# SwiGLU's second product on one Trainium2 core: seven products of halved operands in place of eight, with the operand sums kept in DRAM

## The chip, the cores and the metric

The program runs on one core of one Trainium2 chip. TensorE (PE) multiplies matrices, VectorE (DVE) and ScalarE (ACT) work on elements, GpSimd (POOL) works on elements and issues transfers, and SyncE (SP) issues transfers. The metric is the device time of one execution in microseconds; less is better.

## The reference

One decoder layer on 1024 tokens of width 1024: a mixer sub-layer, a residual with a layer norm, a SwiGLU sub-layer, and a second residual with a layer norm. Only the last part matters here:

```
def swiglu(u, w1, w2):                      # u: 1024 x 1024
    gate, up = jnp.split(u @ w1, 2, axis=-1)   # w1: 1024 x 5632
    return (jax.nn.silu(gate) * up) @ w2       # w2: 2816 x 1024
# y = layer_norm(ALPHA * x1 + g2 * swiglu(u2), ln2_g, ln2_b)
```

All inputs and the output are float32. The kernel holds each operand of a product as a high and a low part (`split`: ScalarE rounds to float32r, VectorE subtracts), and makes a product of three matmuls: high by high, high by low, low by high.

## The kernel before

The mixer sub-layer takes the first 1300 us and is not touched. Then comes a loop over eight token tiles that writes the normed rows to DRAM (`scratch["n1"]`), then SwiGLU.

**SwiGLU's first product** makes the hidden values h, 2816 by 1024 (hidden by tokens), in 22 blocks of 128 hidden units. The first three blocks are plain. Blocks 3 to 21 (the loop at L1180) already use seven products for eight: gate and up, and the two token halves, are the halves of a 2 by 2 scheme. Each of the seven products of a block is 4 x 3 = 12 matmuls of 128x128 by 128x512 (`product`, L1109). Between them ScalarE and VectorE take sums out of PSUM, and `sums` (L1132 to L1137 and the splits) prepares the next block's weights, in six portions. VectorE must read an accumulator before the next product that adds into it, two products later. The hidden values go to `scratch["h"]` in DRAM (L1210, L1214).

**SwiGLU's second product** goes over two groups of 512 tokens. In a group, 22 steps over the hidden blocks each load w2's rows (128x1024, by SP) and h's block (128x512, by ACT's queue), split both, and issue 24 matmuls (`step`, L1231): four token tiles by two halves of the columns by three. The first four steps (`AHEAD`, L1237) are set up while the first product still runs, with tiles of the older pools; those pools are closed behind them and the new pools `f2a`, `f2`, `f2l` take their memory. The last 4 or 6 steps of a group are done token tile by token tile, so that the ends of the rows are spread out. At a row's end VectorE does, for each half, a product with g2, a sum with the residual and `bn_stats` (L1308 to L1311), then `bn_aggr`, and two scalings for each half (L1316, L1320); the row goes out on SP's queue. The residual rows are loaded from `n1` (L1287) and scaled and shifted in VectorE (L1295).

Within a stage the order on each engine is made by a list scheduler when the program is built, by program order among what it takes to be ready; on the chip each engine then keeps to that order. `tc.issue_after(x)` puts an instruction behind x on its engine. A load can be placed ahead of its place in the program when its memory is free.

## Time and profile before

| | us |
|---|---|
| median of three runs (2087.52 to 2092.55) | 2088.6 |
| the profiled execution, its own time | 2079.7 |
| its span, first to last instruction | 2078.0 |
| PE busy | 2015.1 (97%) |
| DVE busy | 1234.6 (59%) |
| ACT busy | 750.8 (36%) |
| POOL busy | 137.3 (7%) |

Busy times are sums over all stages. A matmul's length in the profile (389 ns) is longer than the time between two starts, since matmuls are pipelined. The difference between the time and the span, 1.7 us, lies before the first and behind the last instruction.

### The profile page before, as it was taken

What the parts mean: (1) busy time and instruction counts of PE and PEld (TensorE: products, weight loads), DVE (VectorE), ACT (ScalarE), POOL (GpSimd) and SP (SyncE); (2) the same over time, 40 slices, a digit from 0 to 9 for tenths busy, and PEclk for the clock granted to TensorE, in tenths of its full rate; (3) what the DMA queues carried; (4) which work ended last, traced back from release to release, by engine and by line L of the source; (5) the groups of instructions that cost most, each with busy time, mean ns of one, the idle gap of its engine ahead of it and who ended that gap; (6) DMA issues with size and microseconds to landing.
All of it is one profiled execution on the core that took longest, in us unless ns stands there. A gap on an engine that the chain in (4) does not pass through costs nothing.

```text
span 2078.0 us, 26649 instructions
## 1 busy us (share of the span) xinstructions
PE 2015.1 (97%) x10254; PEld 1588.5 (76%) x10254; DVE 1234.6 (59%) x2323; ACT 750.8 (36%) x1214; POOL 137.3 (7%) x226
## 2 busy tenths in 40 slices
PE   6999999999999899999999999999999999999998
PEld 5777777776777677776776788788888888878886
DVE  6584575565642767447656457654856565445756
ACT  3514323323325433434445323554333333333231
POOL 1101102001001000002112000010000000000000
PEclk9999989999989999999999999999999999999999
DMA  9111111111121445211111565545423222265552
GB/s 294 48 63 37 44 44 46 46 52 46 56 64 56 147 143 163 62 41 32 35 32 41 170 210 166 178 142 171 142 73 92 91 77 76 76 232 178 185 177 75
DMA packets 195311, 213.20 MB, mean 103 GB/s; under 512 B 10588, under 2 KB 146416, under 8 KB 195184
## 3 DMA queue, kind: packets, MB, share of 16 engines
q1 hardware_dynamic: 162672, 139.51, 22.4%
q10 hardware_dynamic: 30400, 66.70, 9.3%
q0 software_dynamic: 2112, 5.29, 0.8%
q8 instruction: 81, 1.33, 0.3%
q14 instruction: 46, 0.38, 0.1%
HBM read 168.45 MB, written 43.00 MB: 102 GB/s over the span
## 4 chain that ended last, share of the span: by engine, by line
PE 77%; DVE 10%; issue 6%; ACT 4%; DMA 3%; POOL 1%; SPq 1%; DVEq 0%; ACTq 0%; POOLq 0%
PE psd L143 20%; PE accf L1231 11%; PE py L1109 7%; PE pj L143 5%; PE px L1109 5%; PE pz L1109 5%; PE woa L1030 3%; PE pgu L143 3%; PE po L871 2%; PE pt L857 2%; DVE tw L478 1%; DVE TI L480 1%; PE pm L463 1%; PE pss L841 1%; PE pw L530 1%
## 5 line engine op out<-in xcount | busy, mean ns | idle before, releaser
L143 PE MATMUL psd<-ul,wh 128*128 128x512 f32 x992 | 337.8, 411 | 0.7 <-DVE ul L274 0.7
L143 PE MATMUL psd<-uh,wh 128*128 128x512 f32 x992 | 334.6, 409 | 0.3 <-ACT wh L118 0.2
L143 PE MATMUL psd<-uh,wl 128*128 128x512 f32 x992 | 332.0, 407 | 1.1 <-DVE wl L120 1.1
L143 PEld LDWEIGHTS psd<-uh,wh 128*128 128x128 f32 x992 | 185.5, 191 | 40.9 <-issue 6.4
L143 PEld LDWEIGHTS psd<-ul,wh 128*128 128x128 f32 x992 | 183.3, 190 | 41.3 <-issue 6.8
L143 PEld LDWEIGHTS psd<-uh,wl 128*128 128x128 f32 x992 | 184.3, 191 | 39.5 <-issue 5.7
L107 ACT ACTIVATE wh<-wraw 128x1024 fp32r<-128x1024 f32 (+1 forms) x89 | 83.9, 943 | 329.6 <-PE psd L143 252.5
L108 DVE TENSOR_TENSOR wl<-wraw,wh 128x1024 fp32r<-128x1024 f32 (+1 forms) x89 | 95.6, 1074 | 66.9 <-ACT wh L107 64.9
L1231 PE MATMUL accf<-w2h,hh 128*128 128x512 f32 x320 | 105.1, 389 | 1.3 <-ACT w2h L107 1.3
L1231 PE MATMUL accf<-w2l,hh 128*128 128x512 f32 x320 | 105.2, 389 | 0.5 <-DVE w2l L108 0.5
L1231 PE MATMUL accf<-w2h,hl 128*128 128x512 f32 x320 | 105.0, 389 | 0.0
L108 DVE TENSOR_TENSOR w2l<-w2raw,w2h 128x1024 fp32r<-128x1024 f32 x44 | 53.7, 1222 | 35.7 <-ACT w2h L107 30.6
L1231 PEld LDWEIGHTS accf<-w2h,hh 128*128 128x128 f32 x320 | 60.0, 188 | 14.0 <-ACT w2h L107 1.7
L1231 PEld LDWEIGHTS accf<-w2l,hh 128*128 128x128 f32 x320 | 60.0, 188 | 13.4 <-DVE w2l L108 1.0
L1231 PEld LDWEIGHTS accf<-w2h,hl 128*128 128x128 f32 x320 | 60.1, 188 | 12.5
L847 ACT ACTIVATE sc<-sc,mx 128x128 f32<-128x128 f32 (+7 forms) x64 | 49.6, 775 | 42.4 <-DVE mx L846 36.5
L849 POOL TENSOR_SCALAR sc<-sc,mx 128x128 f32<-128x128 f32 (+7 forms) x64 | 48.8, 766 | 218.0 <-DVE mx L848 186.6
L534 ACT ACTIVATE UV<-pu 64x64 f32<-64x64 f32 x64 | 13.7, 214 | 136.6 <-PE pu L533 136.4
L143 PE MATMUL pj<-oh,wh 128*128 128x512 f32 x192 | 59.2, 390 | 0.3 <-DVE macc L974 0.3
L143 PE MATMUL pj<-ol,wh 128*128 128x512 f32 x192 | 59.4, 390 | 0.0
L107 ACT ACTIVATE w2h<-w2raw 128x1024 fp32r<-128x1024 f32 x44 | 46.1, 1051 | 36.7 <-DMA w2raw<-in_ffn_w_dram 18.9
L108 DVE TENSOR_TENSOR hl<-hraw,hh 128x512 fp32r<-128x512 f32 x40 | 27.5, 689 | 53.5 <-ACT hh L107 53.4
(457 smaller groups left out, 4188.6 us busy)
## 6 DMA issues: line engine op xcount, KB each, us to landing
wraw<-in_w_in_dram SPq DMA_DIRECT2D x62, 512.0 KB, 3.9
w2raw<-in_ffn_w_dram SPq DMA_DIRECT2D x44, 512.0 KB, 3.7
w1raw<-in_ffn_w_dram SPq DMA_DIRECT2D x38, 512.0 KB, 4.2
wada<-in_w_ada_dram SPq DMA_DIRECT2D x64, 256.0 KB, 2.9
s_gate<-gate ACTq DMA_DIRECT2D x24, 512.0 KB, 2.9
gate<-s_gate ACTq DMA_DIRECT2D x24, 512.0 KB, 4.3
s_h<-ht ACTq DMA_DIRECT2D x44, 256.0 KB, 2.2
hraw<-s_h ACTq DMA_DIRECT2D x44, 256.0 KB, 3.2
```

Of the source, the lines that this page charges most:

```text
L107: S.activation(hi, raw, AF.Copy)
L108: return V.tensor_tensor(lo_, raw, hi.bitcast(F32), OP.subtract).ins
L143: i = mm(ps[:, h * HF:(h + 1) * HF], w[:, k, :], u[k][h], start=(k == 0 and w is wh and u is uh), stop=(k == nk - 1 and w is wl))
L463: mm(pm[hd][:, :, j], BK[hr, c].rearrange("p a b -> p (a b)"), AR[hr, c], start=True, stop=True)
L478: V.tensor_tensor(t3, X[:, s + 1:32, s:s + 1].to_broadcast([64, ni, nj]), TI[:, s:s + 1, 0:nj].to_broadcast([64, ni, nj]), OP.mult)
L847: S.activation(sc[:, 0:n], sc[:, 0:n], AF.Exp, bias=mx[:, 2:3], accum_out=mx[:, 3:4])
L849: G.tensor_scalar(sc[:, 0:n], sc[:, 0:n], mx[:, 4:5], 1.0, op0=OP.mult, op1=OP.mult)
L857: PE.transpose(pt[:, j, :], sc[:, (k0 + j) * P:(k0 + j + 1) * P], ident)
L871: mm(po[hr, q0:2 * P], VT[:, kj, hr], PTs[hd][:, kj, q0:2 * P], start=(kj == 0), stop=(kj == nk - 1))
L1030: mm(acc[:, half(h)], m_[k][h2][:, tl], w_[h], start=(k == 0 and m_ is mh and w_ is wh), stop=(k == KT - 1 and m_ is ml))
L1109: ins = mm(ps, w[i][:, k, :], u[k][j], start=(start and k == 0 and m == 0), stop=(stop and k == 3 and m == 2), skip_group_check=not start)
L1231: mm(acc[t][h], m_[:, t * P:(t + 1) * P], w_[:, half(h)], start=(k == 0 and m_ is hh and w_ is wh), stop=(k == NHB - 1 and m_ is hl))
```

## The change

The second product becomes seven products too. h and w2 are cut in halves: pairs of hidden blocks (m = 0 to 10 gives blocks 2m and 2m+1), token halves and column halves. Each product goes over 11 pairs, with 12 matmuls of 128x512 for a pair (four token tiles by three). The operand sums S1 to S4 (of h) and T1 to T4 (of w2) are made pair by pair by `pair_sums`, called behind the blocks of the first product's loop: four loads, up to four VectorE sums and up to four stores to DRAM, all transfers on POOL's queue. 21 such calls lie behind the blocks 4 to 21 (two calls at 6, 12 and 18), the last (S of pair 10) behind the loop. They are kept in parts of DRAM that are no longer needed; five pairs of T3 have no place and are made in VectorE when needed (`w2less`). `AHEAD` is still four steps, each of 12 matmuls. Two sets of four PSUM banks, X and Y, take turns; `after` takes the sums out of them. The residual rows are now eight tiles, loaded and prepared in the first two products; rows 0 to 3 are finished inside the sixth product, rows 4 to 7 at the end.

```diff
+    places = [scratch[n][q * P:(q + 1) * P, half(h)] for n, nb in (("gate", 24), ("o_a", 4), ("o_b", 4), ("o_c", 4))
+              for q in range(nb) for h in range(2)]
+    places = places[16:] + places[:16]
+    kept = {}
+    for m in range(NPR):
+        kept["S1", m] = scratch["h"][2 * m * P:(2 * m + 1) * P, half(1)]
+    for n in ("T2", "S2", "T1", "S4", "T4", "S3", "T3"):
+        for m in range(NPR):
+            if places:
+                kept[n, m] = places.pop(0)
...
+    def pair_sums(what, m):
+        src = h_part if what == "S" else w2_part
+        q = {}
+        for i in range(2):
+            for j in range(2):
+                q[i, j] = tmp()
+                nc.gpsimd.dma_start(q[i, j], src(2 * m + j, i) if what == "S" else src(2 * m + i, j))
+
+        def op(n, dst, x, y, o=OP.subtract):
+            V.tensor_tensor(q[dst], q[x], q[y], o)
+            if (n, m) in kept:
+                nc.gpsimd.dma_start(kept[n, m], q[dst])
+
+        if what == "S":
+            op("S1", (1, 1), (1, 0), (1, 1), OP.add)
+            op("S3", (1, 0), (0, 0), (1, 0))
+            op("S2", (0, 0), (1, 1), (0, 0))
+            op("S4", (0, 1), (0, 1), (0, 0))
...
+        for n in range(0 if i == NPL else 2 if i % 6 == 0 else 1):
+            if waiting and (waiting[0][0] == "T" or 2 * waiting[0][1] + 1 < i):
+                pair_sums(*waiting.pop(0))
+    for job in waiting + [("S", NPR - 1)]:
+        pair_sums(*job)
...
+    PRODUCTS = (("A11", "B11", "X", True), ("S2", "T2", "Y", True), ("A12", "B21", "X", False),
+                ("S1", "T1", "Y", True), ("S4", "B22", "X", True), ("S3", "T3", "Y", True), ("A22", "T4", "X", True))
...
+    f2a = ctx.enter_context(tc.tile_pool(name="f2a", bufs=5, side="right", reuse_waits="tile"))
...
+        def operands(a_, b_, m, pool):
+            raw = f2a.tile([P, HF], F32, name="w2raw", bufs=3)
+            if (b_, m) in kept or b_ in B:
+                nc.sync.dma_start(raw, kept[b_, m] if (b_, m) in kept else B[b_](m))
+            else:
+                less = f2a.tile([P, HF], F32, name="w2less", bufs=1)
+                nc.sync.dma_start(raw, w2_part(2 * m + 1, 1))
+                nc.sync.dma_start(less, w2_part(2 * m, 1))
+                V.tensor_tensor(raw, raw, less, OP.subtract)
+            wh, wl = (pool.tile([P, HF], F32R, name="w2" + n) for n in "hl")
+            split(raw, wh, wl)
+            raw = f2a.tile([P, HF], F32, name="hraw", bufs=3)
+            nc.scalar.dma_start(raw, A[a_](m) if a_ in A else kept[a_, m])
...
+        def add_up(t, h, src, other=None):
+
+            c_ = word()
+            if other is not None:
+                V.tensor_tensor(c_, src, other, OP.add)
+                src = c_
+            V.tensor_tensor(c_, src, g2row[:, half(h)], OP.mult)
+            V.tensor_tensor(rows_of[t][:, half(h)], rows_of[t][:, half(h)], c_, OP.add)
+            V.bn_stats(stats[t][:, h, :], rows_of[t][:, half(h)])
...
+        def after(p, acc, t):
+            if p == 0:
+                S.activation(U[t], acc[t], AF.Copy)
+            elif p == 1:
+                V.tensor_tensor(U[t], acc[t], U[t], OP.add)
+            elif p == 2:
+                add_up(t, 0, acc[t])
+            elif p == 3:
+                V.tensor_tensor(U4[t], acc[t], U[t], OP.add)
+            elif p == 4:
+                add_up(t, 1, acc[t], U4[t])
+            elif p == 5:
+                V.tensor_tensor(U[t], acc[t], U[t], OP.add)
+                add_up(4 + t, 1, acc[t], U4[t])
+            else:
+                add_up(4 + t, 0, acc[t], U[t])
+                finish_row(4 + t)
...
+            end = NPR - LATE if p == 6 else NPR
+            for m in range(AHEAD if p == 0 else 0, end):
+                ops = operands(a_, b_, m, f2a)
                 for t in range(4):
...
+                if p == 0 and m == AHEAD + 1:
+                    g2row, g_r, b_r, ag, ab = (load_row(f2, src, 0, n) for src, n in names)
+                n = NPR * p + m - AHEAD - 2
+                if n in range(8):
+                    nc.sync.dma_start(rows_of[n], scratch["n1"][n * P:(n + 1) * P, :])
                 with tc.issue_after(behind[-1]):
...
+                    if p == 5 and m - 4 in range(4):
+                        finish_row(m - 4)
+            if p < 6:
+                for t in range(4):
+                    after(p, acc, t)
+            else:
+                ops = [operands(a_, b_, m, f2l) for m in range(end, NPR)]
+                for t in (0, 2, 1, 3):
+                    for m in range(end, NPR):
+                        step(acc, t, ops[m - end], False, m == NPR - 1, True)
+                    after(p, acc, t)
```

`LATE` is 6 and `NPR` is 11. `finish_row` holds the same `bn_aggr`, square root, reciprocal, four scalings and two stores as the row's end before.

## Rows read from the trace of the kernel before

**Rows 1.** Page, busy time, share of the span and instructions of an engine.
```profile
PE 2015.1 (97%) x10254; PEld 1588.5 (76%) x10254; DVE 1234.6 (59%) x2323; ACT 750.8 (36%) x1214; POOL 137.3 (7%) x226
```

**Rows 2.** The chain that ended last: start, length, engine, tile, line, count.
```profile
1811.01 2.72 PE px L1109 x12
...
1827.33 21.32 PE accf L1231 x94
1851.61 209.32 PE accf L1231 x922
```

**Rows 3.** Windows: stretch, its length, busy time by engine, granted clock, DMA share, GB/s.
```profile
1522.50:1541.50 19.00, 19.00 (x85) 15.73 (x84) 11.57 (x17) 6.42 (x10) 0.00 (x0) 1.00 0.27 83
...
2000.00:2040.00 40.00, 40.00 (x178) 33.13 (x177) 21.51 (x23) 14.40 (x18) 0.00 (x0) 1.00 0.50 158
...
2068.90:2078.00 9.10, 0.17 (x1) 0.00 (x0) 5.82 (x11) 0.29 (x1) 0.00 (x0) 0.65 0.19 75
```

**Rows 4.** Timeline of DVE in block 8 of the first product: start, length, instruction, idle before.
```profile
1560.81 0.69 DVE L1212 TENSOR_TENSOR c<-c,py 128x512 f32<-128x512 f32 x1 [0.64 <-PE py L1109]
1561.53 0.69 DVE L1213 TENSOR_TENSOR ht<-ht,c 128x512 f32<-128x512 f32 x1
...
1566.89 0.69 DVE L1132 TENSOR_TENSOR s<-w1raw 128x512 f32<-128x512 f32 x1 [2.18 <-DMA w1raw<-in_ffn_w_dram]
1567.50 0.68 DVE L1190 TENSOR_TENSOR c<-c 128x512 f32<-128x512 f32 x1
1568.11 0.69 DVE L1133 TENSOR_TENSOR s<-s,w1raw 128x512 f32<-128x512 f32 x1
```

**Rows 5.** Timeline of DVE at the end: the last row of the output.
```profile
2069.69 0.67 DVE L1308 TENSOR_TENSOR t1f<-accf,g2row 128x512 f32<-128x512 f32 x1
2070.40 0.69 DVE L1310 TENSOR_TENSOR t1f<-x1r,t1f 128x512 f32<-128x512 f32 x1
2071.12 0.69 DVE L1311 BATCH_NORM_STATS2 st<-t1f 128x6 f32<-128x512 f32 x1
2071.85 0.21 DVE L1313 BATCH_NORM_AGGREGATE mv<-st 128x2 f32<-128x12 f32 x1
...
2073.49 1.41 DVE L1320 SCALAR_TENSOR_TENSOR t1f<-t1f,mv,l2b 128x512 f32<-128x512 f32 x2
```

**Rows 6.** Groups by line from 1851 us on: count, busy time, mean ns, idle before.
```profile
L107 ACT ACTIVATE hh<-hraw 128x512 fp32r<-128x512 f32 x38 | 23.9, 629 | 80.7 <-PE accf L1231 52.3 <-DMA hraw<-s_h 28.2
...
L1295 DVE TENSOR_TENSOR x1r<-x1r,l1g 128x1024 f32<-128x1024 f32 x8 | 9.8, 1220 | 0.0
```

**Rows 7.** Timeline of PE where the second product's new pools begin.
```profile
1848.47 0.61 PE L1231 MATMUL accf<-w2h,s4l 128*128 128x512 f32 x2
1850.35 0.73 PE L1231 MATMUL accf<-w2h,hh 128*128 128x512 f32 x2 [1.26 <-ACT w2h L107]
1851.61 0.73 PE L1231 MATMUL accf<-w2l,hh 128*128 128x512 f32 x2 [0.53 <-DVE w2l L108]
```

**Rows 8.** Timeline of SP's queue about the start of the second product.
```profile
1805.01 19.37 SPq L1239 DMA_DIRECT2D w2raw<-in_ffn_w_dram  x2
1824.46 8.72 SPq L1287 DMA_DIRECT2D x1r<-s_n  x4
1835.36 36.01 SPq L1264 DMA_DIRECT2D w2raw<-in_ffn_w_dram  x9
```

**Rows 9.** Windows in the same stretch, columns as in rows 3.
```profile
1827.00:1830.00 3.00, 3.00 (x15) 2.49 (x14) 1.38 (x2) 0.00 (x0) 0.00 (x0) 1.00 1.00 356
...
1833.00:1836.00 3.00, 3.00 (x14) 2.46 (x14) 1.23 (x1) 0.87 (x1) 0.00 (x0) 1.00 1.04 418
```

**Rows 10.** DMA issues, KB each and us to landing, and POOL's own time for one.
```profile
hraw<-s_h ACTq DMA_DIRECT2D x44, 256.0 KB, 3.2
s_gate<-ut POOLq DMA_DIRECT2D x16, 256.0 KB, 2.7
...
L1055 POOL DMA_DIRECT2D s_gate<-ut x16 | 12.1, 756 | 248.4 <-ACT oh L1052 208.0 <-ACT uh L1052 40.5
```

**Rows 11.** Waits between 1465 and 1827 us: total, times, longest.
```profile
DVE s L1132 <- DMA w1raw<-in_ffn_w_dram: 35.8, 15, 3.3
```

More of the change, by code (lines that the diff above doesn't have):

```diff
@@ L1065, in trunk @@
     NPL = 3
+    LATE = 6
     def banks(i):
@@ L1178, in fourth, with h_part, w2_part @@
             split(t2f[k], *T4[k])
+    NPR = NHB // 2
+    places = [scratch[n][q * P:(q + 1) * P, half(h)] for n, nb in (("gate", 24), ("o_a", 4), ("o_b", 4), ("o_c", 4))
[8 more added lines that the diff above has]
+                kept[n, m] = places.pop(0)
+    def h_part(k, h):
+        return scratch["h"][k * P:(k + 1) * P, half(h)]
+    def w2_part(k, h):
+        return w2[k * P:(k + 1) * P, half(h)]
+    def pair_sums(what, m):
[15 more added lines that the diff above has]
+        else:
+            op("T1", (0, 0), (0, 1), (0, 0))
+            if ("T3", m) in kept:
+                op("T3", (0, 1), (1, 1), (0, 1))
+            op("T2", (1, 1), (1, 1), (0, 0))
+            op("T4", (1, 0), (1, 0), (1, 1))
+    waiting = [("T", m) for m in range(NPR)]
+    for m in range(NPR - 1):
+        waiting.insert(min(2 * m + 3, len(waiting)), ("S", m))
     for i in range(NPL, NHB):
@@ L1225, in accumulators, with banks_of, step @@
+    for job in waiting + [("S", NPR - 1)]:
+        pair_sums(*job)
+    def banks_of(which):
+        if which == "X":
+            both = [pso.tile([P, T], F32, name="accx", tag=t) for t in ("o1", "o0")]
+        else:
+            both = [pso.tile([P, T], F32, name="accy", tag="o2")]
+        acc = [b[:, half(h)] for b in both for h in range(2)]
+        while len(acc) < 4:
+            acc.append(pso.tile([P, HF], F32, name="accz", tag="t", bufs=2))
         return acc
-    def step(acc, k, t, ops, halves=(0, 1)):
+    def step(acc, t, ops, start, stop, fresh):
@@ L1228, in step @@
         wh, wl, hh, hl = ops
-        for m_, w_ in ((hh, wh), (hh, wl), (hl, wh)):
-            for h in halves:
-                mm(acc[t][h], m_[:, t * P:(t + 1) * P], w_[:, half(h)],
-                   start=(k == 0 and m_ is hh and w_ is wh), stop=(k == NHB - 1 and m_ is hl))
-    acc = accumulators()
+        for n, (m_, w_) in enumerate(((hh, wh), (hh, wl), (hl, wh))):
+            mm(acc[t], m_[:, t * P:(t + 1) * P], w_, start=(start and n == 0), stop=(stop and n == 2),
+               skip_group_check=not fresh)
@@ L1236, in trunk @@
     AHEAD = 4
-    for k in range(AHEAD):
-        raw = wpool.tile([P, D], F32, name="w2raw", tag="wraw")
-        nc.sync.dma_start(raw, w2[k * P:(k + 1) * P, :])
-        wh, wl = (wpool.tile([P, D], F32R, name="w2" + m, tag="w" + m) for m in "hl")
+    for m in range(AHEAD):
+        raw = wpool.tile([P, HF], F32, name="w2raw", tag="wraw")
+        nc.sync.dma_start(raw, B["B11"](m))
+        wh, wl = (wpool.tile([P, HF], F32R, name="w2" + n, tag="w" + n) for n in "hl")
         split(raw, wh, wl)
@@ L1242, in trunk @@
         raw = gpool.tile([P, HF], F32, name="hraw", tag="gate")
-        nc.scalar.dma_start(raw, scratch["h"][k * P:(k + 1) * P, half(0)])
-        hh, hl = (f1.tile([P, HF], F32R, name=f"s{(2, 1, 3, 4)[k]}{m}") for m in "hl")
+        nc.scalar.dma_start(raw, A["A11"](m))
+        hh, hl = (f1.tile([P, HF], F32R, name=f"s{(2, 1, 3, 4)[m]}{n}") for n in "hl")
         split(raw, hh, hl)
@@ L1247, in trunk @@
             for t in range(4):
[L1248 removed]
+                step(X, t, (wh, wl, hh, hl), m == 0, False, True)
     f1_ctx.close()
     uctx.close()
[L1251 to L1288 removed]
@@ L1289, in trunk @@
                 with tc.issue_after(behind[-1]):
-                    if grp == 0 and k - k0 == 4:
+                    if n == 3:
                         for r in (ag, ab):
                             V.tensor_scalar(r, r, ALPHA, None, op0=OP.mult)
-                    if k - k0 - 5 in range(8):
-                        t, m = divmod(k - k0 - 5, 2)
-                        V.tensor_tensor(x1s[t], x1s[t], (ag, ab)[m], (OP.mult, OP.add)[m])
-            ops = [operands(k, f2a if k >= NHB - 2 else f2l) for k in range(NHB - late, NHB)]
```

110 lines of the change are left out of this document (42 added, 68 removed).

## The prediction

> **What bounds the kernel now.** I read the busy times first: PE is busy for 97% of the span and VectorE for 59% [rows 1]. A mean over stages says little, so the chain that ended last comes next. In SwiGLU it is nothing but PE: groups of 12 matmuls every 2.72 us (0.2267 us a matmul), and the second product is two pieces of the chain, from 1827.33 and from 1851.61 us, to the last matmul at about 2068.9 [rows 2]. The windows then show how much the others have left. In a block of the first product VectorE is busy 11.57 of 19.0 us and ACT 6.42; in the second product VectorE is busy 21.51 of 40 us; behind the last matmul come 9.1 us that PE does not share in [rows 3]. So fewer matmuls are worth their full price as long as VectorE, the loads and the end keep up. The question is whether they do.
>
> **PE's part.** Before: 2 groups x 22 steps x 24 = 1056 matmuls. After: 7 products x 11 pairs x 12 = 924, of the same 128x512 form. 132 fewer at 0.2267 us are **29.9 us less**. A product takes 132 x 0.2267 = 29.9 us, a pair 2.72 us. That fewer are issued follows from the loops, so the change does what it says; what is open is what waits in between.
>
> **VectorE's price for an operation.** An operation on 128x512 that does not need the one before it starts 0.60 us after it (1567.50 to 1568.11); one that needs it starts 0.72 us after it (1560.81 to 1561.53) [rows 4]. A row's end from `bn_aggr` to the last scaling lasts from 2071.85 to 2074.90, 3.05 us, or 2.96 us if the next operation overlaps its end by the 0.09 us that 0.69 us of length and 0.60 us of pitch differ by; from there to the span's end are 3.1 us (the last store) [rows 5]. A 1024-wide operation on a residual row is 1.22 us [rows 6].
>
> **VectorE in the seven products.** A pair needs two low parts, 1.2 us of its 2.72. To this come the sums out of PSUM. For the first product ACT takes them. Second: 4 operations. Third: 4 x 3. Fourth: 4. Fifth: 4 x 4. Sixth: 4 x 5. Seventh: 4 x 4. The 16 residual operations lie in the second product mostly (11 of them): 22 x 0.60 + 11 x 1.22 = 26.6 of 29.9 us, so this still fits, barely. Products three to five have 13.2 us of splits and at most 12 x 0.72 = 8.6 us of sums: they fit. The last two do not. From the end of the fifth product on, VectorE has still to do: the fifth's sums, 16 x 0.72 = 11.5 us; the sixth's low parts, 14 x 0.60 = 8.4 us (five operand buffers let about four pairs be ready ahead); five T3 sums, 3.0 us; the ends of rows 0 to 3, 4 x 2.96 = 11.8 us; the seventh's low parts, 22 x 0.60 = 13.2 us; the sixth's sums, 4 x 0.60 + 16 x 0.72 = 13.9 us; and four rows of 4 x 0.72 + 2.96 = 5.84 us each, 23.4 us. Together 85.2 us. The first sums can start three token tiles (9 matmuls, 2.0 us) before the product ends, and the store adds 3.2 us: 86.4 us. PE alone would take 2 x 29.9 us and before's end of 9.1 us: 68.9 us. **VectorE is thus the bound of the last two products, by 17.5 us.** This is the upper bound if VectorE never waits. If all 48 chained sums find another operation to stand between them, each saves 0.12 us and the excess is 11.7 us. I take 15, nearer the upper one, since the four last rows have little to interleave and VectorE must wait here for a tile of PE's. Work can't be done much earlier to help: the seventh's operands go through the same three raw buffers as the sixth's, which are filled in program order. Some of the 15 us are PE waits in the sixth product (each of the pairs 4 to 7 has a row's end queued on VectorE behind its split, so the next pair's split stands behind 2.96 us), some at the start of the seventh (the sixth's 20 sums come before the splits from the pairs not yet ready), and the rest is the end: four rows 5.84 us apart against 18 matmuls, 4.08 us, for a token tile.
>
> **The start of the second product.** Before, PE loses 2.1 us where the old pools end (the next step would have been due 0.23 us after the last of 96, at 1849.1; the first ones run at 1850.35 and the rest from 1851.61, two matmuls further) [rows 7]. The cover was the four steps ahead, 21.8 us; it is now 4 x 2.72 = 10.9 us. Behind it lie on SP's queue the residual rows: four loads stood ahead of the first new w2 load and took it until 1835.36, 8 us into the second product [rows 8]. Now eight rows can take that place. They and the five broadcast rows are 13 x 0.524 = 6.8 MB. The engines moved at most 418 GB/s, with their share at 1.0, in this stretch [rows 9]: 6.8 MB are 16.3 us at that. If all of it comes first and begins 2 us before the second product, the first new load lands some 16.3 - 2 + 3 us in, and with ACT's and VectorE's split (1.3 us) PE waits until 18.6 us instead of 10.9: a loss near 8 us. With S of pair 10, whose loads wait for the last block's h and whose VectorE sums stand ahead of new splits on VectorE, it can be 15 us. If the new loads come first, the loss is that of before or none. I take 6 us, 4 more than before; bounds -2 and +13. By Perfetto Trace Analysis of the Trainium skill, section Roofline, one core's transfers end at about 435 GB/s; the 418 here agree, and by it the burst would be 15.7 us and the loss 0.6 us less.
>
> **The first product.** A call of `pair_sums` is four VectorE operations, about 0.72 x 4 = 2.9 us, so VectorE comes to 14.5 us of 19.0 in a block with one call and 17.4 us with two [rows 3]. POOL did nothing here; seven or eight transfers at 0.756 us are 6 us of it, and 256 KB landed in 2.7 us from its queue [rows 10]. DMA rises from 83 GB/s by 2 MB in 19 us, 110 GB/s, still half of the peak. Cost nothing, under the cover of the slack that an eviction has: two products, 5.44 us, less its own 0.69. If that cover is used up, see the third rival. Scratch tiles are ten, of which the block's own sums need four and a call four; I see no wait there that exceeds a block. The stores to DRAM are needed a product or more later, so hidden.
>
> **ACT** has two high parts (0.63 us each [rows 6]) and one issue for a pair, 1.6 of 2.72 us: no bound.
>
> **Sum.** -29.9 + 15 + 4 + 0 = **-10.9 us**. On the profiled execution's 2079.7 us this gives 2068.8, a span of 2067. The median of the runs is 2088.6, 8.9 us above that execution, and the time that is predicted is a median: **2077.7 us**. With the bounds 11.7 to 17.5 and -2 to +7 the case itself reaches from 2068 to 2083.
>
> **Rivals.** (1) VectorE's work is hidden after all, since the order drawn up at build time puts row ends and low parts into its free time (in products three to five it has some 8 to 13 us each). Against it stand the buffers. Then only one operation more at the end and the start cost: -29.9 + 0.7 + 2 = -27, 2061 us. (2) The start is starved: VectorE and SP stand behind S of pair 10 and the eight rows, loss 15 instead of 6 us: 2086.7 us, about no change. For it speaks that four rows did stand ahead before. (3) It gets slower in the first product. VectorE keeps its order; a pair's first sum that stands before an eviction holds it until POOL's four loads have landed. VectorE already waits 2.4 us on average, at most 3.3, for w1's loads there, without harm to PE [rows 11]; that is 15 waits of 35.8 us in all. A pair needs four issues of 0.756 and a landing of 2.7 us, 5.7 us if its tiles come free late, and then 2.9 us of sums behind it: more than the 4.7 us of slack. At 1 us lost for each of 21 calls, +21 - 10.9: 2098.7 us. It becomes slower by over 0.3% from 0.82 us a call. TensorE: Matmul & The Clock Gate of the Trainium skill, section on the array's architectural detail, calls ACT's and VectorE's queues strict FIFO; by that rule the time would be this rival's if the loads are late, and the waits of rows 11 agree with it.
>
> **Chances.** Forecast 0.53, rival (1) 0.10, (2) 0.17, (3) 0.20. A measurement of this kernel tells 0.3%, 6.3 us, from no change. Of the forecast's case 0.45 lie below 2082.3 and 0.08 above; (1) is faster; (2) is 0.13 the same and 0.04 slower; (3) is 0.17 slower and 0.03 the same. Faster 0.55, same 0.24, slower 0.21. The range leaves half of the first rival and half of the third out: 2063 to 2099.
>
> **What would show it.** The first product's groups of 12 in the chain stay 2.72 us apart; if not, (3). The gap behind the first 48 matmuls is near 6 us. In products two to five PE has no waits of note. In the sixth and seventh PE waits for low parts of VectorE, some 5 us in each, VectorE is busy for over 90% from the fifth product's end on, and from the last matmul to the end are about 14 us instead of 9.1. If VectorE idles there and PE does not wait, the forecast's main term is wrong; if these 15 us are there but the first product has gaps, the sum is wrong by (3) alone.

## The result and the profile after

The changed kernel takes 2106.1 us (median of four runs, 2100.12 to 2107.78) against 2088.95 us for the kernel before on the same chip: a ratio of 1.0077 [1.0060, 1.0095], 0.8% slower. The forecast was 2077.7 us, faster, with a range up to 2099: wrong in sign and outside the range. The profiled execution took 2100.12 us, its span is 2098.4 us against 2078.0. The profiled execution of e12 ran at a granted clock of 0.556 (3258.1 us) and is compared with nothing here; e13 is the same kernel.

The first line of the page, beside [rows 1]:

```profile
PE 1995.3 (95%) x10122; PEld 1566.3 (75%) x10122; DVE 1312.9 (63%) x2501; ACT 770.1 (37%) x1284; POOL 229.8 (11%) x397
```

There are 132 matmuls less, as counted, and PE is busy 20 us less. Part of the other 10 us of the 29.9 went where the clock fell behind gaps, as the windows show. They are cut at stages: first product, steps ahead, the gap at the start, the rest of the first of the seven products with the second to the fifth, sixth, seventh, end (columns as in [rows 3]).

```profile
1464.90:1835.40 370.50, 363.79 (x1597) 298.99 (x1596) 260.45 (x401) 120.57 (x193) 88.71 (x164) 1.00 0.61 198
1835.40:1846.50 11.10, 11.07 (x49) 8.82 (x47) 2.77 (x4) 1.26 (x2) 1.60 (x3) 1.00 0.98 360
1846.50:1866.00 19.50, 1.21 (x2) 0.57 (x2) 3.93 (x6) 2.27 (x5) 2.17 (x4) 0.58 0.89 348
1866.00:2006.40 140.40, 140.40 (x611) 115.94 (x611) 100.48 (x149) 63.38 (x112) 0.00 (x0) 0.99 0.63 203
2006.40:2042.10 35.70, 30.83 (x124) 23.83 (x123) 32.51 (x60) 12.24 (x22) 0.00 (x0) 0.95 0.61 197
2042.10:2083.60 41.50, 35.92 (x142) 27.63 (x140) 36.38 (x62) 11.74 (x22) 0.00 (x0) 0.92 0.36 121
2083.60:2098.40 14.80, 0.13 (x1) 0.00 (x0) 10.52 (x20) 0.59 (x2) 0.00 (x0) 0.67 0.28 107
```

PE idles 6.7 us of 370.5 in the first product, works 1.2 of 19.5 us at the start, loses nothing in products two to five, and idles about 5 us in each of the last two. One table for all kernels of this study, in us, read from PE's timeline: from the first matmul of block 3 to the first of the second product; from there to the end of the first of the seven, with the gap at the new pools in it; the four products after it; the last two; from the last matmul to the end.

| kernel | first product | start, 1st | 2nd to 5th | 6th, 7th | end | sum | ratio to before |
|---|---|---|---|---|---|---|---|
| before | 361.8 | 241.7 for all eight | | | 9.1 | 612.6 | 1 |
| after | 370.5 | 51.3 | 119.6 | 77.1 | 14.8 | 633.5 | 1.0077 |
| e1 no calls | 361.8 | 50.0 | 119.6 | 77.7 | 13.9 | 623.0 | 1.0050 |
| e2 late S | 369.8 | 48.0 | 119.6 | 79.7 | 14.8 | 632.0 | 1.0089 |
| e3 T3 kept | 371.0 | 48.6 | 119.6 | 74.1 | 13.6 | 626.9 | 1.0101 |
| e4 rows raw | 369.5 | 51.3 | 119.6 | 72.8 | 14.3 | 627.6 | 1.0080 |
| e5 rows spread | 373.5 | 40.3 | 120.7 | 80.1 | 14.6 | 629.2 | 1.0109 |
| e6 start | 376.6 | 37.1 | 120.2 | 79.4 | 14.1 | 627.5 | 1.0065 |
| e7 held | 361.8 | 53.8 | 119.6 | 80.2 | 13.8 | 629.2 | 1.0076 |
| e8 relief | 373.2 | 48.8 | 119.6 | 92.2 | 13.2 | 647.2 | 1.0163 |
| e9 six early | 369.6 | 48.3 | 121.1 | 78.3 | 13.1 | 630.6 | 1.0102 |
| e10 all | 361.8 | 30.8 | 132.1 | 78.0 | 13.5 | 616.2 | 1.0016 |
| e13 six first | 373.6 | 48.7 | 120.6 | 64.2 | 14.9 | 622.0 | 1.0046 |
| e11 order | 361.8 | 34.5 | 127.5 | 63.8 | 15.7 | 603.2 | 0.9960 |
| e14 spread | 361.8 | 33.3 | 127.1 | 67.3 | 15.1 | 604.7 | 0.9963 |

A product of PE alone is 29.9. The table begins at block 3 because the untouched mixer in front ended anywhere from 1464.9 to 1479.0 us in these executions, which is more than most stages differ by. Against before, the 20.9 us of after are -29.9 (PE), +8.8 (first product), +19.3 (start: 51.3 - 29.9, less the 2.1 of before), +17.3 (77.1 - 59.8) and +5.7 (end), which is 21.2; the 0.3 between them come from rounding and from where the stages are cut. These are the two profiled executions; the medians differ by 17 us.

**The first product.** What PE waited for, 1485 to 1830 us (total, times, longest; before has no such line):

```profile
PE py L1110 <- DVE c L1249: 4.4, 3, 2.1
PE py L1110 <- ACT c L1237: 1.8, 3, 1.0
PE pz L1110 <- DVE c L1244: 0.5, 1, 0.5
```

One of these places, first in VectorE's timeline, then in POOL's:

```profile
1637.44 0.69 DVE L1133 TENSOR_TENSOR s<-w1raw 128x512 f32<-128x512 f32 x1
1641.45 0.69 DVE L1211 TENSOR_TENSOR s<-s 128x512 f32<-128x512 f32 x1 [3.33 <-DMA s<-in_ffn_w_dram]
1642.06 0.68 DVE L1263 TENSOR_TENSOR c<-c,py 128x512 f32<-128x512 f32 x1
```

```profile
1634.69 0.54 POOL L1213 DMA_DIRECT2D s_o_a<-s  x1 [0.19 <-issue]
1635.23 0.54 POOL L1208 DMA_DIRECT2D s<-in_ffn_w_dram  x1
...
1636.95 0.54 POOL L1208 DMA_DIRECT2D s<-in_ffn_w_dram  x1 [0.46 <-DMA s_gate<-s]
```

The sum of a T pair (L1211) stands on VectorE before the eviction of `py` (L1263) and waits 3.33 us for a load that POOL could issue only after the stores of the S pair before it (1635.23). The eviction comes 4 us late. It reaches PE here by way of ACT:

```profile
1643.98 0.33 ACTq L1265 DMA_DIRECT2D s_h<-ht  x1
1644.35 0.60 ACT L1237 ACTIVATE c<-py 128x512 f32<-128x512 f32 x1 [5.74 <-PE pz L1110]
```

```profile
1645.00 0.50 PE L1110 MATMUL py<-uh,s3h 128*128 128x512 f32 x1 [0.44 <-ACT c L1237]
```

Behind the late eviction VectorE makes the block's last hidden values (L1264), ACT's queue holds their store (L1265), and behind that store stands ACT's own eviction of the next block's accumulator (L1237), for which PE waits. Of the seven waits of PE listed above three are for this eviction of ACT, behind the same store each time, four for one of VectorE's own (`DVE c`). It is the third rival's mechanism. Spread over the calls it is 8.8 / 21 = 0.42 us, in place of 1, but it is not spread: VectorE waited for loads at these sums at 27 places, 58 us in all, and PE lost time at seven places only, 0.6 to 2.4 us each with the slower starts behind a wait. The other waits lay under the slack. In the kernels below that leave the calls as they are, the first product took 369.5 to 376.6 us, so that its loss is 8 to 15 us; why it varies is open. The page TensorE: Matmul & The Clock Gate of the Trainium skill, section on the array's architectural detail, has VectorE's queue as strict FIFO; these lines agree.

**The start.** SP's queue, POOL's, then VectorE's:

```profile
1833.59 11.69 SPq L1402 DMA_DIRECT2D x1r<-s_n  x8
1847.77 8.20 SPq L1323 DMA_DIRECT2D w2raw<-in_ffn_w_dram  x3
```

```profile
1843.80 1.60 POOL L1208 DMA_DIRECT2D s<-s_h  x3 [22.60 <-DMA s_h<-ht]
```

```profile
1841.80 0.69 DVE L108 TENSOR_TENSOR w2l<-w2raw,w2h 128x512 fp32r<-128x512 f32 x1 [2.09 <-ACT w2h L107]
1855.40 2.87 DVE L1211 TENSOR_TENSOR s<-s 128x512 f32<-128x512 f32 x4 [12.91 <-DMA s<-s_h]
1864.84 0.69 DVE L108 TENSOR_TENSOR w2l<-w2raw,w2h 128x512 fp32r<-128x512 f32 x1 [6.56 <-ACT hh L107]
```

And ACT's first high part of a new pair:

```profile
1863.53 0.63 ACT L107 ACTIVATE w2h<-w2raw 128x512 fp32r<-128x512 f32 x1 [21.76 <-DMA s_o_b<-s]
```

All eight rows stand before the first new w2 load ([rows 8] had four), which landed 12.2 us after its issue, at about 1860.0. The S sums of pair 10 stand before the first new split on VectorE, and the profile puts the end of ACT's wait to a store of these sums: the new tiles take the memory in which the sums lay. So by this trace two chains end some 3.5 us apart, and the longer one goes through pair 10, whose own loads shared the DMA engines with the burst. The DMA engines were full (share 0.98) at 360 GB/s. PE's clock fell to 0.58 in the gap; 18.25 us of the 21.4 are the wait, the other 3 slower starts behind it.

**The last two products.** The longest idle times of PE, with what ended them:

```profile
2033.92 0.73 PE L1287 MATMUL accy<-w2l,hh 128*128 128x512 f32 x1 [1.69 <-DVE w2l L108]
2041.32 0.50 PE L1287 MATMUL accy<-w2h,hh 128*128 128x512 f32 x1 [0.76 <-ACT w2h L107]
2055.83 1.22 PE L1287 MATMUL accx<-w2l,hh 128*128 128x512 f32 x2 [5.58 <-DVE w2l L108]
```

VectorE is busy 32.5 of 35.7 and 36.4 of 41.5 us there (91 and 88%, where over 90% was forecast), with the end 79.4 of 92.0; the longest wait of PE lies behind the sixth product's 20 sums. PE's waits are 10.5 of the 17.3 us lost in these two products. The other 6.8 are matmuls that started more slowly behind a wait: the granted clock was 0.95 and 0.92 in the two windows.

### The profile page after: what moved, and what is told of

It reads as the page before. It is cut to its first block, busy times and chain, and to the rows that moved or that the text cites. A ratio compares the mean times of both kernels' runs of the same rounds, so it can differ in the third digit from the quotient of the medians.

```text
span 2098.4 us, 27280 instructions
## 1 busy us (share of the span) xinstructions
PE 1995.3 (95%) x10122; PEld 1566.3 (75%) x10122; DVE 1312.9 (63%) x2501; ACT 770.1 (37%) x1284; POOL 229.8 (11%) x397
## 4 chain that ended last, share of the span: by engine, by line
PE 68%; DVE 13%; DMA 7%; issue 5%; ACT 4%; POOL 1%; SPq 1%; DVEq 0%; POOLq 0%; ACTq 0%
PE psd L143 21%; PE pj L143 6%; PE py L1110 5%; PE accx L1287 4%; PE woa L1030 3%; PE pgu L143 3%; PE pz L1110 3%; PE px L1110 3%; PE po L871 2%; DMA s<-in_ffn_w_dram 2%; PE pt L857 2%; DVE tw L478 1%; DVE TI L480 1%; PE accz L1287 1%; PE accy L1287 1%
## 5 line engine op out<-in xcount | busy, mean ns | idle before, releaser
L108 DVE TENSOR_TENSOR wl<-wraw,wh 128x1024 fp32r<-128x1024 f32 (+1 forms) x89 | 95.6, 1074 | 67.7 <-ACT wh L107 65.7
L1211 DVE TENSOR_TENSOR s<-s 128x512 f32<-128x512 f32 x83 | 57.3, 690 | 72.5 <-DMA s<-in_ffn_w_dram 43.9
L1287 PE MATMUL accx<-w2h,hh 128*128 128x512 f32 x160 | 64.2, 402 | 18.3 <-ACT hh L107 18.3
L107 ACT ACTIVATE w2h<-w2raw 128x512 fp32r<-128x512 f32 x77 | 47.9, 624 | 72.8 <-DMA s_o_b<-s 22.0
L108 DVE TENSOR_TENSOR w2l<-w2raw,w2h 128x512 fp32r<-128x512 f32 x77 | 52.9, 689 | 32.5 <-ACT w2h L107 25.7
L849 POOL TENSOR_SCALAR sc<-sc,mx 128x128 f32<-128x128 f32 (+7 forms) x64 | 48.8, 766 | 218.0 <-DVE mx L848 186.6
L107 ACT ACTIVATE hh<-hraw 128x512 fp32r<-128x512 f32 x73 | 45.7, 627 | 71.3 <-DMA hraw<-s_h 18.5
L1287 PE MATMUL accx<-w2l,hh 128*128 128x512 f32 x160 | 64.5, 404 | 5.6 <-DVE w2l L108 5.6
L108 DVE TENSOR_TENSOR hl<-hraw,hh 128x512 fp32r<-128x512 f32 x73 | 50.1, 689 | 24.3 <-ACT hh L107 24.3
L1287 PE MATMUL accx<-w2h,hl 128*128 128x512 f32 x160 | 64.2, 403 | 0.0
L1110 PE MATMUL px<-oh,wh 128*128 128x512 f32 x152 | 59.1, 389 | 0.0
```

What stands on the lines that cost most here:

```text
L107: S.activation(hi, raw, AF.Copy)
L108: return V.tensor_tensor(lo_, raw, hi.bitcast(F32), OP.subtract).ins
L849: G.tensor_scalar(sc[:, 0:n], sc[:, 0:n], mx[:, 4:5], 1.0, op0=OP.mult, op1=OP.mult)
L1110: ins = mm(ps, w[i][:, k, :], u[k][j], start=(start and k == 0 and m == 0), stop=(stop and k == 3 and m == 2), skip_group_check=not start)
L1211: V.tensor_tensor(q[dst], q[x], q[y], o)
L1287: mm(acc[t], m_[:, t * P:(t + 1) * P], w_, start=(start and n == 0), stop=(stop and n == 2), skip_group_check=not fresh)
```

## The experiments

**e1: the 21 calls inside the first product left out** (their sums are not made, so the later products read what DRAM held).

```diff
-        for n in range(0 if i == NPL else 2 if i % 6 == 0 else 1):
-            if waiting and (waiting[0][0] == "T" or 2 * waiting[0][1] + 1 < i):
-                pair_sums(*waiting.pop(0))
```

> Leaves out the 21 calls of pair_sums inside the first product's loop (the second product then reads old contents of DRAM); the call for S of pair 10 behind the loop stays. Theory (VectorE keeps its order and stands in front of evictions until POOL's loads land): the 8.7 us that the first product lost are gone, its groups of 12 are 2.72 us apart throughout; the gap of 18 us in the second product and the slow sixth and seventh products stay; about 9 us (0.4%) less than the changed kernel. Rival (the first product loses time through the greater DMA traffic of which these calls are only a part, or through something else in the change): less than half of the 8.7 us comes back.

The ratio is 1.0050 [1.0031, 1.0069], the first product 361.8 us with no wait of PE. The calls cost the whole 8.8 us of the first product, and nothing else in it does.

**e7: the sums held behind the block's last eviction** (`end_`), loads and stores left in place.

```diff
+                q = pair_loads(*job, tmp, nc.gpsimd)
+                with tc.issue_after(end_):
+                    pair_ops(*job, q)
```

> In the first product the four sums of each of the 21 calls are held on VectorE behind their block's last eviction; loads and stores stay as they are. Theory (VectorE stands in front of evictions because the sums are placed by an estimate of when their loads land, and POOL's loads, queued behind stores and scratch tiles, land later): most of the 8.7 us is gained back, under 3 us lost. Rival (the ten scratch tiles are too few, and w1's own sums wait for the calls' stores): the loss stays at 6 us or grows.

The first product is 361.8 us again, with all its transfers and all its VectorE work. It was the order, not the load on an engine. VectorE's timeline, with no wait at a sum:

```profile
1638.17 0.69 DVE L1270 TENSOR_TENSOR ht<-ht,c 128x512 f32<-128x512 f32 x1
1638.78 0.68 DVE L1214 TENSOR_TENSOR s<-s 128x512 f32<-128x512 f32 x1
...
1639.98 0.69 DVE L1214 TENSOR_TENSOR s<-s 128x512 f32<-128x512 f32 x1
...
1641.28 1.41 DVE L1214 TENSOR_TENSOR s<-s 128x512 f32<-128x512 f32 x2
```

The time, 1.0076 [1.0033, 1.0119], did not follow: the start (53.8) and the last two (80.2) were longer by 5.6 us together, and the 4.3 us by which its sum is less lie within the interval.

**e2: S of pair 10 called behind pair 6 of the first of the seven products**, in tiles of its own.

```diff
-    for job in waiting + [("S", NPR - 1)]:
+    for job in waiting:
...
+                if p == 0 and m == AHEAD + 2:
+                    pair_sums("S", NPR - 1, word)
```

> Moves the call for S of pair 10 from behind the loop into the first of the seven products, behind its pair 6, with tiles of the new pool (cm) instead of the old pool's scratch tiles. Theory (the 18 us gap is the chain of this call: the last block's h lands, POOL loads, four VectorE sums, four stores, and only then are the scratch tiles free that the new operands lie in): the gap falls to 2 to 6 us, some 13 to 16 us (0.7%) less than the changed kernel. Rival (the eight residual rows and five broadcast rows fill the transfers and keep the new operands away): the gap stays above 9 us, at most 9 us less.

48.0 us at the start in place of 51.3, ratio 1.0089 [1.0056, 1.0122]: the theory that pair 10 alone starves the start fell. But the scheduler had drawn its loads (1833.87 us) and sums (1856.9) forward again, so the edit moved less than it meant to: the sums no longer hold the new tiles' memory, but VectorE still makes them before its first new split.

**e5: each row load and broadcast row held behind a given pair's load** (the rows at pairs 6, 8, 10, 12, 30, 32, 34 and 36, counted through the seven products).

```diff
+                with tc.issue_after(loads_sp[-1]):
+                    if k in ROW_AT:
+                        nc.sync.dma_start(rows_of[t], scratch["n1"][t * P:(t + 1) * P, :])
```

> Holds the loads of the eight residual rows and of the five broadcast rows behind the operand loads of given pairs (one row every second pair, rows 4 to 7 only in the fourth product); S of pair 10 stays behind the first product's loop. Theory, formed again after the move of S of pair 10 alone brought 3 us: two chains end at nearly the same time in that gap, S of pair 10 and the 6.8 MB of rows that come ahead of the new operands; taking the rows away leaves S of pair 10 on quiet queues: last block's h lands 2.5 us after its store, POOL's loads 4.3, sums 2.9, stores 4.8, split 1.3, so a gap of 5 to 8 us instead of 18.5. Rival (S of pair 10 alone sets it, whatever the traffic): 14 us or more.

40.3 us: without the burst 11 of the 21 us lost at the start come back. Ratio 1.0109 [1.0063, 1.0154], since the first product was 3 us longer and the last two as well. **e6** holds pair 10 back as well: its loads on ACT's queue behind pair 7, its sums behind pair 9.

```diff
+                if k == 7:
+                    with tc.issue_after(loads_act[-1]):
+                        last_s = pair_loads("S", NPR - 1, word, nc.scalar)
+                if k == 9:
+                    with tc.issue_after(behind[-1]):
+                        pair_ops("S", NPR - 1, last_s)
```

> As the run with the rows spread, and S of pair 10 too: its loads stand on ACT's queue behind the operands of pair 7 of the first of the seven products, its sums behind VectorE's low parts of pair 9. Theory (both chains together are the whole gap): 1 to 4 us remain, as before the change (2.1), since the new operands' tiles still lie in those of the steps ahead; the first of the seven products loses under 5 us instead of 21. Rival (the short cover of four half steps, 10.9 us, is itself too short for the new loads): more than 6 us remain.

37.1 us, 7.2 over a product where less than 5 was expected; ratio 1.0065 [1.0039, 1.0091]. In that product PE waits twice for a high part of h, 4.1 us in all. ACT's timeline there:

```profile
1858.29 0.33 ACTq L1338 DMA_DIRECT2D hraw<-s_h  x1
1858.65 5.52 ACTq L1208 DMA_DIRECT2D cm<-s_h  x3
1865.03 0.63 ACT L107 ACTIVATE hh<-hraw 128x512 fp32r<-128x512 f32 x1 [6.16 <-DMA hraw<-s_h]
...
1865.49 0.36 ACTq L1338 DMA_DIRECT2D hraw<-s_h  x1
...
1870.45 0.63 ACT L107 ACTIVATE hh<-hraw 128x512 fp32r<-128x512 f32 x1 [2.87 <-DMA hraw<-s_h]
```

Pair 10's four loads (`cm`) stand together between two loads of h: the one in front lands late beside them, the one behind is issued only after them. The rival's words, over 6 us left, came true, but its mechanism, a cover too short, did not: e10 brings the product to 30.8 us with the same cover.

**e3: five more places in DRAM, so that all of T3 is kept.**

```diff
+    places = places[16:] + places[:16] + [scratch["t3"][q * P:(q + 1) * P, :] for q in range(5)]
```

> Keeps T3 of all eleven pairs (five more places in DRAM); no sum of w2 is made in the sixth product. Theory (VectorE's whole work from the fifth product's end on is the bound): 5 x 0.6 us less work, so the end comes about 3 us earlier (0.15%), PE's waits in the sixth product shrink but return at the seventh's start. Rival (the single w2less tile, whose load, sum and next load follow one another at about 4.7 us a pair, sets the sixth product's pace): the sixth product loses under 1 us instead of 5.8 and the end comes 5 us or more earlier.

The last two products and the end fell by 4.2 us, between the two forecasts; the ratio, 1.0101 [1.0058, 1.0144], doesn't show it. **e4: rows 0 to 3 written out without their norm** (the ends of four rows left out).

```diff
-                        finish_row(m - 4)
+                        for h in range(2):
+                            nc.sync.dma_start(y[(m - 4) * P:(m - 3) * P, half(h)], rows_of[m - 4][:, half(h)])
```

> Leaves out the ends of rows 0 to 3 in the sixth product (bn_aggr, square root, reciprocal, four scalings; the rows go out unscaled), 4 x 2.96 = 11.8 us of VectorE's work. Theory (VectorE's whole work is the bound to the end): the end comes 10 to 12 us earlier (0.5%), of which less than 6 lie in the sixth product itself. Rival (only the sixth product's waits come from it; the seventh product and the end have their own limits): 4 to 6 us earlier.

About 12 us of VectorE's work taken away gave back 4.8 (the ratio is 1.0080 [1.0053, 1.0108]): the rival. A sum of VectorE's work that sets the end would have given back nearly all.

**e8: T3 kept, rows 0 to 3 ended by ACT and POOL, the last six pairs made in the sixth product.**

```diff
+                S.activation(t1[:, half(h)], t1[:, half(h)], AF.Identity, scale=mv[:, 2:3], bias=mv[:, 3:4])
+                G.tensor_tensor(t1[:, half(h)], t1[:, half(h)], g_r[:, half(h)], OP.mult)
+                G.tensor_tensor(t1[:, half(h)], t1[:, half(h)], b_r[:, half(h)], OP.add)
```

> Keeps T3 of all pairs, gives the scaling of rows 0 to 3 to ACT (normalising) and POOL (gain and shift, 1.3 us each), with the stores on POOL's queue, and prepares the last six pairs' operands of the seventh product, which have tiles of their own, inside the sixth. VectorE has 3.0 + 10.6 us less to do and 7.2 us are moved forward. Theory (from the fifth product's end on VectorE's work in its order is the bound): sixth product within 1.5 us of 29.9, seventh and end together 44 to 47 us instead of 56, so 15 to 17 us less than the changed kernel there. Rival (three raw buffers and the loads' latency set the pace when VectorE has room): the seventh product keeps over 5 us of waits.

It got slower, 1.0163 [1.0125, 1.0201], the last two 92.2 us, with a wait of PE of 10.0 us in the seventh (the rival's sign). VectorE, then POOL:

```profile
2028.10 0.20 DVE L1010 BATCH_NORM_AGGREGATE mv<-st 128x2 f32<-128x12 f32 x1
2028.22 1.67 DVE L108 TENSOR_TENSOR w2l<-w2raw,w2h 128x512 fp32r<-128x512 f32 x1
...
2030.00 2.43 DVE L1013 SCALAR_TENSOR_TENSOR mv<-mv 128x1 f32<-128x1 f32 x1
...
2035.92 6.14 DVE L108 TENSOR_TENSOR w2l<-w2raw,w2h 128x512 fp32r<-128x512 f32 x2
```

```profile
2027.53 1.82 POOL L1372 TENSOR_TENSOR x1r<-x1r,l2g 128x512 f32<-128x512 f32 x1
...
2034.16 1.28 POOL L1372 TENSOR_TENSOR x1r<-x1r,l2g 128x512 f32<-128x512 f32 x1
2035.37 0.58 POOL L1374 DMA_DIRECT2D out_dram<-x1r  x1
2035.97 1.28 POOL L1373 TENSOR_TENSOR x1r<-x1r,l2b 128x512 f32<-128x512 f32 x1
```

While POOL's operations followed each other, two splits of VectorE took 6.14 us, where two take 1.28 otherwise. From the fifth product's end on VectorE was busy 79.7 us, as long as in after, though 13.6 us of its work were taken away. That is not all of the 92.2 us: VectorE also idles 12.8 us in front of the last rows, as it does in e9 without POOL.

**e9: T3 kept, and the seventh product's last six pairs made in the fifth** (behind its pairs 1, 2, 4, 5, 7 and 8), without POOL.

```diff
+                if NPR * p + m in LATE_AT:
+                    late_ops.append(operands("A22", "T4", NPR - LATE + len(late_ops), f2l))
```

> T3 kept, as in the run with five more places, and the operands of the seventh product's last six pairs made within the fifth product, one pair behind each of six pairs, where VectorE is about half idle. Theory (VectorE's sum of work from the fifth product's end sets the end): 12 splits of 0.69 us less after it, so the last two products and the end take 87.7 - 8.3, about 79 to 81 us, and the fifth product grows by at most 1 us. Rival (the latency of loads that wait for their raw buffers sets the pace of the last two): no more than 3 us less, 85 to 88 us. In both the start and the first product stay as in the changed kernel (370 and about 49 us), the span behind block 3 about 619 to 621 by the theory and 624 to 627 by the rival, against 612.6 before.

91.4 us for the last two and the end, 3.7 more than e3: both forecasts missed. VectorE's sum alone does not set the end of this kernel. Its timeline says what does (the sixth product's sums are L1380 to L1352, the splits L108):

```profile
2053.24 0.68 DVE L1380 TENSOR_TENSOR u<-accy,u 128x512 f32<-128x512 f32 x1
...
2064.61 0.69 DVE L108 TENSOR_TENSOR w2l<-w2raw,w2h 128x512 fp32r<-128x512 f32 x1
...
2068.22 0.69 DVE L108 TENSOR_TENSOR hl<-hraw,hh 128x512 fp32r<-128x512 f32 x1
2080.01 0.69 DVE L1348 TENSOR_TENSOR cm<-accx,u 128x512 f32<-128x512 f32 x1 [11.11 <-PE accx L1287]
```

```profile
2065.36 1.22 PE L1287 MATMUL accx<-w2l,hh 128*128 128x512 f32 x2 [8.13 <-DVE w2l L108]
```

PE waits 8.13 us for a split that stands behind 12 us of sums; then VectorE has nothing to do for 11.11 us, while PE works off the rest of the first five pairs and then starts on the six that had been ready all the time. The two engines take turns where they should overlap.

**e12 and e13 (one kernel): the seventh product begins with the six early pairs**, and the other five follow, token tile by token tile.

```diff
+            for m in range(LATE) if p == 6 else ():
+                for t in range(4):
+                    step(acc, t, late_ops[m], m == 0, False, True)
...
+                ops = [operands(a_, b_, m, f2a) for m in range(end)]
```

> The run with the six operands made in the fifth product, with one thing more: the seventh product begins with those six pairs and ends with the five others, operand by operand for one token tile after the other. Theory (not VectorE's sum but the order on its queue: the sixth product's evictions, 12 us, stand before the splits that TensorE needs next): 16 us of TensorE's work that needs nothing from VectorE now lies over the evictions; the wait of 8.1 us and the low clock behind it go, and the last two products and the end take 79 to 84 us for 91.4; the rest as in that run (start 48, four products of 30 to 31). Rival (loads that wait for their raw buffers set the pace): the five last pairs are loaded no sooner, 88 us or more.

Its ratio was 1.0040 [1.0024, 1.0056]. The stages are those of e13.

> The kernel whose seventh product begins with the six early pairs, again, for a profile at full clock: where the 0.6 per cent that it gained come from. Theory (order on VectorE's queue): no wait of TensorE over 3 us behind the sixth product's evictions (8.1 us in the run without the swap), VectorE not idle for 11 us in front of the last rows, last two products and the end 79 to 84 us. Rival (something in front of them, the start or the fifth product, gained it): last two products and the end 88 or more.

1.0046 [1.0027, 1.0064], the last two and the end 79.1 us, 12.3 less than e9; the ratios differ by 0.0056, 11.7 us. The longest wait of PE from 1990 us on lies in the sixth product, and none over 0.4 us behind that product's sums:

```profile
PE accy L1287 <- DVE w2l L108: 2.6, 1, 2.6
```

The work is that of e9 on every engine; only the order in which PE takes the pairs is new. From the fifth product's end to the end of the span, e9 first, then e13 (columns as in [rows 3]):

```profile
2013.70:2105.20 91.50, 65.69 (x265) 51.62 (x264) 71.85 (x128) 19.43 (x36) 0.00 (x0) 0.87 0.34 117
```

```profile
2011.40:2090.60 79.20, 61.34 (x265) 49.02 (x264) 71.58 (x128) 19.46 (x36) 0.00 (x0) 0.93 0.38 134
```

VectorE is busy 71.9 of 91.5 us and 71.6 of 79.2. So its sum is not refuted as a floor: the new order comes near it, and 79 to 81 us is what e9's theory had forecast from that sum. What e9 lacked was the order that lets VectorE work almost without a pause.

**e10: e7's hold, e3's places, six early pairs as in e9 but one of them in the fourth product, rows from pair 12 on, pair 10's loads one behind a pair on SP's queue.**

```diff
+                    if k in range(7, 11):
+                        i, j = divmod(k - 7, 2)
+                        last_s[i, j] = word()
+                        nc.sync.dma_start(last_s[i, j], h_part(2 * (NPR - 1) + j, i))
```

> All remedies at once: sums held behind the block's last eviction, the loads of pair 10's S sums one behind each of four pairs on SP's queue and their sums at the tenth pair after them, the eight rows and the five broadcast rows one behind a pair from the twelfth pair on, T3 kept, the seventh product's last six pairs made in the fourth and fifth. Theory (three separate losses, each with its own cause): first product 361.8 us; start and first of the seven products 32 to 35; four products of 30 each; last two products and the end 78 to 82; the span behind block 3 592 to 599 against 612.6 before, ratio to before 0.990 to 0.9935. Rival (the losses are one shortage of VectorE or of transfers that only moves): what is taken out at the start comes back in the second to fifth products (over 31 us each) or at the end (over 87), the span behind block 3 at 605 or more, ratio 0.997 or more.

Ratio 1.0016 [1.0001, 1.0031], sum 616.2: the rival's side. First product and start have lost nearly nothing (361.8, 30.8), but the rows' VectorE work, with the third product's sums, now lay before the fourth product's splits, and that product took 36.7 us. The last two and the end took 91.5, as in e9, where the theory had 78 to 82. **e11** adds the order of e13, puts rows 0 to 3 into the second product and rows 4 to 7 into the fourth and fifth, and makes all six early pairs in the fifth.

```diff
-        ROW_AT = (15, 17, 19, 21, 24, 26, 28, 30)
+        ROW_AT = (11, 13, 15, 17, 35, 37, 39, 41)
```

> All remedies at once with two changes of order: the seventh product begins with its six early pairs, and the work on the eight rows is placed where VectorE is idle: rows 0 to 3 within the rest of the first and the second product, rows 4 to 7 in the fourth and fifth. Theory (order on VectorE's queue): the wait of 4.3 us at the start of the fourth product goes, so the four products take 30 to 31 each; the last two and the end 77 to 83; start and first of the seven 31 to 33; first product 361.8. Span behind block 3 590 to 600 against 612.6 before, ratio 0.980 to 0.9935 (the level of the untouched part in front varies by some us). Rival (VectorE's sum or the transfers): rows brought forward make the start late again (36 or more), or the last two and the end stay at 88 or more; span behind block 3 at 605 or more, ratio 0.996 or more.

2077.8 us against 2085.4, ratio **0.9960 [0.9941, 0.9979]**: faster than both kernels, by 0.4% than before and, by the two ratios, 1.2% than after. Its sum, 603.2, is between the two forecasts, 9.4 us less than before of the 29.9 that PE has less to do. The first product (361.8) and the last two with the end (79.5) came as the theory had them; the start (34.5 for 31 to 33) and the four products (127.5 for 120 to 124) did not. Windows of its fifth product (1952.6 to 1989.7), from 3 us in front of it to the end of its last wait, and the rest:

```profile
1949.40:1979.70 30.30, 25.92 (x112) 20.53 (x112) 22.93 (x35) 16.19 (x28) 0.00 (x0) 1.00 0.76 248
1979.70:1990.00 10.30, 10.30 (x38) 8.06 (x38) 6.16 (x11) 5.60 (x11) 0.00 (x0) 0.83 0.71 244
```

The fifth product takes 37.0 us (waits, then a clock of 0.83). **e14** spreads the six early pairs and gives h a fourth raw buffer.

```diff
-        late_ops, LATE_AT = [], (46, 47, 48, 50, 51, 52)
+        late_ops, LATE_AT = [], (40, 43, 46, 48, 50, 52)
```

> All remedies with both changes of order, the six early pairs spread over the fourth and fifth products with two or three pairs between them in place of one, and a fourth buffer for the raw halves of h. Theory (in the fifth product the loads of the early pairs take raw buffers and so delay its own: TensorE waited 3.4 us for hh and ran some us at the low clock): the fifth product takes 30 to 31.5 for about 36, the span behind block 3 595 to 600 for 603.2, ratio 0.992 to 0.9945. Rival (the wait only moves to the fourth product, whose VectorE queue is full): 602 or more, ratio 0.9955 or more.

0.9963 [0.9944, 0.9982], the fifth product 34.9 us, the sum 604.7: the rival's numbers, the wait only moved, though not to the fourth product (31.2 us) but to the sixth, which took 37.3 us in place of 32.7. Whether the raw buffers or VectorE's queue hold the fifth product stays open.

## Why the prediction was wrong

**PE's part: right.** Products two to five take 29.9 us each, and 132 matmuls are gone.

**VectorE's price of an operation: right.** 0.60 us of pitch; pairs of independent ones are listed as 1.28 us for two.

**The start: the step that failed most.** The text took 6 us of loss, with bounds of -2 and +13 over before, and only up to +7 in the range of its own case, for which it gives no reason; the loss was 21.4, 19.3 over before, beyond both. "If all of it comes first" was the case at hand, with "S of pair 10" on top: the rows first on SP, pair 10 first on VectorE. The burst was priced at the DMA engines' 418 GB/s; 360 was what they gave here, and pair 10's loads and stores went through it too. Each of the two had to be taken away for the start to recover: 51.3 to 40.3 without the burst, 37.1 with pair 10 held too, 30.8 with its loads one at a time and the rows later. This is the second rival, larger than the 15 us at which it was priced.

**The first product: priced at nothing, cost 8.8 us.** "Cost nothing, under the cover of the slack that an eviction has" was wrong, and the third rival right in mechanism, at 8.8 us in place of 21. The slack covers VectorE's work (e7), and most of its waits for POOL's loads, but not all of them in front of an eviction: at seven places it was used up. The rival's own condition, a load that comes late, was met where POOL's queue sent a pair's stores before the next pair's loads.

**The last two products and the end: 15 forecast, 23.0 measured.** The text had the mechanism (the sixth's 20 sums come before the splits), and its signs came close: waits of PE of 4.9 and 5.6 us for "some 5 us in each", 14.8 us of end for "about 14". The step that failed is "VectorE is thus the bound", with its condition "if VectorE never waits". VectorE's work was 79.4 us, less than the 85.2 reckoned, but it took 92.0 us to get through it: 8.4 us of idle time lie between its operations, which the text put at nothing, and 4.2 behind the last. On PE's side the term put at nothing is the 6.8 us of slower starts behind its waits; the text took 0.2267 us for every matmul. The runs say that it is the order that keeps VectorE from its sum: 12 us of work less gave 4.8 (e4), six pairs made early gave nothing (e9), and another order of the same work gave 12.3 (e13).

The forecast's sum comes to +21.2 us with the measured terms (-29.9 + 8.8 + 19.3 + 23.0). Three errors of one sign: each time, work or transfers that fit into free time were taken as free, and where they would stand in a queue was not asked.

## What to carry to other kernels

Before you count added work as hidden, name the instruction behind it on its in-order queue and what that one holds up: here 27 waits of VectorE, busy 63% of the span, cost PE 8.8 us at seven places, and with the sums held behind the block's last eviction that stage lost nothing. When an engine looks like the bound of a stage, see if it idles later in that stage; if so, reorder the consumer so that what is ready runs while the producer is busy, before you take work away; once it no longer idles (e13), its work is near the length of the stage. Transfers for later stages belong behind the next stage's first loads, one at a time, and a burst that is moved must be priced with everything else that is released at the same moment.

## What the runs showed of the hardware

VectorE was held up beside POOL (e8): with POOL's 128x512 operations of 1.28 us back to back, a split took 1.67 us, two took 6.14, and an operation on 128x1 took 2.43 where it takes 0.16 otherwise. One of POOL's took 1.82. A `bn_aggr`, which reads one input, took its 0.20 us in the middle of that one. The page SBUF — State Buffer of the Trainium skill, section "SBUF: two separate sides", says that the two share one pair of ports as an exclusive lock, for VectorE's operations with two SBUF inputs; VectorE's slowed ones have two such inputs, and they agree.

A wait of PE costs more than its length: after 3.43 us without work in e11, starts of matmuls lay 0.43 us apart, in place of 0.23, for another 2.6 us (1980.81 to 1983.37), at a granted clock of 0.57 (1979.70 to 1983.40). In the last two products of after, waits of 10.5 us cost 17.3. In the 19.5 us gap of after the granted clock was 0.58, near the lower of the two levels, 1.2 GHz.
